# The first attention loads and row-maximum pieces placed inside the projections of a hybrid encoder layer

## The chip, the cores and the metric

The kernel runs on one NeuronCore of one Trainium2 chip. The metric is the device time of one execution in microseconds (us); less is better. TensorE (PE) multiplies, VectorE (DVE), ScalarE (ACT) and GpSimd (POOL) do the elementwise work, and SyncE (SP) issues nearly all DMA transfers from one in-order queue.

## The reference

One encoder layer runs on a prompt (1024 tokens) and on a sample (2048 tokens), each of width 1024, with 256 memory tokens each. Cut to what matters:

```python
h = rms_norm(x, norm_pre);  z = h @ w_in          # 1024 -> 2304 columns
u_pool, g_pool, q, k, v, g_attn, q_x, g_x = split(z)
pool_out = multiscale_pool(u_pool, pool_w, pool_scale) * silu(g_pool)      # windows 2, 4, 8, 16
q = apply_rope(rms_norm(q, q_norm));  k = apply_rope(rms_norm(k, k_norm))  # 8 query, 2 key heads of 64
attn_out = softmax(q @ k.T / 8) @ v * silu(g_attn)
k_m, v_m = split(rms_norm(mem, mem_norm) @ w_mem_kv)
x_out = softmax(q_x @ k_m.T / 8) @ v_m * silu(g_x)                         # 4 heads
y = concat(pool_out, attn_out, x_out) @ w_out
return x + rms_norm(y, norm_post)
```

All arithmetic is float32. The kernel reaches that on TensorE by splitting an operand into a high and a low part and adding three products (high by high, high by low, low by high).

## The kernel before, in words

**Phase 1, the projections (L72 to L427).** The tokens go through in super blocks `SB`: the memory tokens, the prompt (two blocks of 512 tokens), and two super blocks of two blocks each for the sample. For a super block the columns of `w_in` come in six groups of up to 384 columns, in the order of the list `tok_groups` (L377): `group_n0` (query heads), `ct[2]` (two gate chunks and the first memory-query chunk), `group_n1` (two query heads, keys, values), `ct[0]` (two pooling chunks and a gate chunk), `ct[1]` (gates), `ct[3]` (second memory-query chunk, two gate chunks). A `transposed` chunk makes 128 columns for 512 tokens by 24 matmuls into a PSUM tile `pz`; `natural` makes tokens by columns. Query and key heads are normalised, rotated on VectorE and POOL (`norm_rope`) and transposed on TensorE (`ptq`). Every result is stored to scratch in DRAM: queries (`dq`, `dqx`), keys (`dk`, `dkm`), values (`dv`, `dvm`), gates (`dg`, from tiles `gst`), pooled values (`dp`).

**Phase 2, attention and output (L430 to L878).** It opens pools of its own when the pools of phase 1 close. A *pair* is 256 queries (two tiles of 128); eight pairs of the sample are followed by four of the prompt. Each pair has three *groups*, of kind 0 and 1 (self attention, one key head each) and kind 2 (memory attention). A *slot* handles one chunk of 128 keys of one group. In a slot `weights` makes S by matmuls with the high part (`qa`, `KA`) and the low part (`qb`, `KB`), and ScalarE takes the exponential into a tile `P`; `sums` adds `P` to `z` (the sum over key chunks, so far 128 x 1024), columns up to `CUT` = 512 on POOL and the rest on VectorE (L613); `values` multiplies `P` by `V` into `acc`. At a group's end `totals` (L631) adds `z` over partitions by matmuls with `ones` into a PSUM tile `N`, `take` multiplies `acc` by the gate, `inverse` takes 1/z and sends it through DRAM (`rows`) to a broadcast tile `gz`, and `store_mix` (L657) multiplies on POOL (`o`, or `pu` for the pooled part), casts the high part of `mix` on ScalarE and subtracts the low part on POOL (L784).

The exponential needs a bound for each row beforehand. `largest` (L553) makes it in pieces, called *looks* here: the high-part product of 128 queries with 1024 keys into a PSUM tile `N`, reduced by VectorE (L570). When a group's pieces are through, `shift` (L574) transposes the negated maxima into a row of `qb`, so that S comes out shifted. A look stands some slots ahead of the slot that needs it; those that fall before slot 0, 20 pieces, are executed before it (L836 to L841).

The output projection of a finished pair is cut into pieces of three matmuls (L726 to L728), spread over the following slots (`HOLD` says when they may start). `Output` loads the rows of x (`xr`, L711), normalises, adds, and stores. For the last pair everything runs at the end. The table of what is due in which slot is written by hand; each engine's instructions stay in the order in which phase 2 writes them (`manual_schedule`). Phase 1's order is the scheduler's, and a tile in a reused place waits for the readers of what was there.

Of the kernel before, what the change touches and what calls it, by code (L numbers as in the profile page):

```python
# [23 lines left out]
def encoder(ctx, tc, I, O):  # L24
# [46 lines left out]

    with ExitStack() as p1:  # L72
# [3 lines left out]
        pst = p1.enter_context(tc.tile_pool(name="pst", bufs=2, space=PSUM))  # L76
# [15 lines left out]
        def hT_block(sb, blk):  # L92
# [4 lines left out]
            for i in range(4):  # L97
                x = two.tile([128, D], F32, name="x", tag="x", bufs=4)
                nc.sync.dma_start(out=x, in_=rows(sb, blk, i))
                if kind not in gains:  # L100
                    gains[kind] = one.tile([128, D], F32, name="gain", tag="gain")
                    src = I["mem_norm" if kind == "mem" else "norm_pre"]
                    nc.sync.dma_start(out=gains[kind], in_=src.broadcast_to([128, D]))
                junk = one.tile([128, D], mybir.dt.bfloat16, name="junk", tag="junk")
                ss = two.tile([128, 1], F32, name="ss", tag="ss")
                nc.scalar.activation(out=junk, in_=x, func=AF.Square, accum_out=ss)
                r = rsqrt(two, ss, 1, D, "rsx")
# [27 lines left out]
        def product(ps, terms):  # L135

            n = len(terms)
            for c, (sh, sl, mh, ml) in enumerate(terms):
                nc.tensor.matmul(ps, lhsT=sh, rhs=mh, start=c == 0, stop=False)  # L139
                nc.tensor.matmul(ps, lhsT=sh, rhs=ml, start=False, stop=False)  # L140
                nc.tensor.matmul(ps, lhsT=sl, rhs=mh, start=False, stop=c == n - 1)  # L141

# [9 lines left out]
        def transposed(hT, w, col):  # L152
# [3 lines left out]
            product(ps, [(w[0][:, c, f], w[1][:, c, f], hT[0][:, c], hT[1][:, c]) for c in range(NC)])  # L156
# [5 lines left out]
        def rope_tables():  # L162
            out = []
            raw = [two.tile([128, NTT, 64], F32, name="ropec", tag="ropec", bufs=1),
                   two.tile([128, NTT, 64], F32, name="ropes", tag="ropes", bufs=1)]
            for r, key in zip(raw, ("rope_c", "rope_s")):
                nc.sync.dma_start(out=r, in_=I[key])
            for key in ("k_norm", "q_norm"):
                g = one.tile([128, 2, 64], F32, name="hg", tag="hg" + key)
# [9 lines left out]
                for j in range(2):  # L179
                    if key == "q_norm":  # L180
                        t = raw[j]
                    else:
                        t = one.tile([128, NTT, 64], F32, name="ropek", tag=f"ropek{j}")
# [7 lines left out]
        def norm_rope(ps, parts, tt):  # L191
# [3 lines left out]
            z = two.tile([128, 384], F32, name="z", tag="z")  # L195
            sq = two.tile([128, 384], F32, name="sq", tag="sq")
            t1 = two.tile([128, 384], F32, name="t1", tag="t1")
            nc.scalar.copy(out=z[:, 0:w], in_=ps[:, 0:w])
            nc.scalar.activation(out=sq[:, 0:w], in_=ps[:, 0:w], func=AF.Square)
            ss = two.tile([128, 6], F32, name="ssh", tag="ssh")  # L200
# [3 lines left out]
            r = rsqrt(two, ss[:, 0:n], n, 64, f"rsh{n}")  # L204
# [22 lines left out]
        def heads_transposed(src, npair):  # L227
# [4 lines left out]
            o = two.tile([128, 2, 3, 128], F32R, name="qst", tag="qst")  # L232
# [7 lines left out]
        def group_n0(s, b, hT, w):  # L240
            if not rope:
                rope.update(zip("qk", rope_tables()))
# [10 lines left out]
        def group_n1(s, b, hT, w):  # L253
            for i in range(4):
                tt = 4 * b + i
                ps = natural(hT, w, i, 0, 384)
                vst = two.tile([128, 2, 64], F32, name="vst", tag="vst")
# [104 lines left out]
        def chunks_group(chunks):  # L362
            def run(s, b, hT, w):
                for k, (_, f, args) in enumerate(chunks):
                    f(s, b, *args, transposed(hT, w, 128 * k))
# [11 lines left out]
        tok_groups = [(w_in, [(512, 384)], group_n0), ct[2], (w_in, [(896, 384)], group_n1),  # L377
                      ct[0], ct[1], ct[3]]
# [12 lines left out]
        def mem_v(s, b, hT, w):  # L391
            for i in range(4):
                ps = natural(hT, w, i, 0, 256).rearrange("p (h d) -> p h d", d=64)
                vst = two.tile([128, 4, 64], F32, name="vmst", tag="vmst", bufs=1)
# [15 lines left out]

        for sb, (kind, s, nb, b0) in enumerate(SB):
            groups = groups_of(sb)
            nxt = []
            for gi, (src, pieces, run) in enumerate(groups):
# [15 lines left out]
    with ExitStack() as p2:  # L430
        def pool(name, bufs, space=bass.MemoryType.SB):
            return p2.enter_context(tc.tile_pool(name=name, bufs=bufs, space=space, reuse_waits="tile"))

        one = pool("p2one", 1)
        two = pool("p2two", 2)
        pss = pool("pss", 2, PSUM)
        psn = pool("psn", 2, PSUM)
        psa = pool("psa", 1, PSUM)
        pso = pool("pso", 1, PSUM)

        ones = one.tile([128, 32], F32, name="ones")
        nc.vector.memset(ones, 1.0)

        KA = [one.tile([128, 2048], F32R, name=f"KA{kind}") for kind in range(2)]
        KB = [one.tile([128, 2048], F32R, name=f"KB{kind}") for kind in range(2)]
        KA.append(one.tile([128, 2, 2, NMEM], F32R, name="KA2"))
        KB.append(one.tile([128, 2, 2, NMEM], F32R, name="KB2"))
        for t in KB:  # L450
            nc.vector.memset(t[64:65].bitcast(F32), 1.0)
        V = [one.tile([128, 16, 64], F32, name=f"V{kind}") for kind in range(2)]
        V.append(one.tile([128, 2, 4, 64], F32, name="V2"))
        has_K, has_V = set(), set()

        def load_K(s, kind):
            has_K.add((s, kind))
            for hl in range(2):
                for t, h in ((KA, 64 * hl), (KB, 0))[:2 - hl]:
                    if kind == 2:  # L460
                        src = DKM[hl, :, :, s].rearrange("d (c j) m -> d c j m", j=2)
                        nc.sync.dma_start(out=t[2][h:h + 64].bitcast(F32), in_=src)
                        continue
# [457 lines left out]
```

## Time and profile before

| | us |
|---|---|
| three runs | 1940.56, 1941.95, 1943.42 |
| median | 1941.95 |
| profiled execution, its own time | 1940.45 |
| span of the profiled execution | 1938.6 |
| TensorE busy | 1830.0 |
| VectorE busy | 1126.4 |
| ScalarE busy | 699.3 |
| POOL busy | 914.3 |

The span is what the profile covers, from the first to the last instruction; the execution's own time is 1.85 us longer. The page divides the span into 40 slices of 48.5 us and gives the busy tenths of each engine and the clock that TensorE was granted. A bracket behind an instruction of the timeline gives the idle time of its engine before it and what ended that time. Engines that are not the bound may be idle at no cost.

### The profile page before, as it was taken

Reading aid. Unit: us, or ns where it says so; the run is one execution under the profiler, and the core shown is the slowest. Engines: PE = TensorE matmul, PEld = TensorE weight load, DVE = VectorE, ACT = ScalarE, POOL = GpSimd, SP = SyncE. Lnnn points to the kernel's source line nnn. Section 1 sums busy time; section 2 is a strip of 40 time slices with the busy share of each in tenths; the row PEclk is TensorE's granted clock in tenths of the full one; section 3 lists DMA queues with packets and bytes.
Section 4 is the critical chain, followed back from the end, with each engine's and each line's share of the span. In section 5 each row is a group of like instructions: output and inputs, shape, how many; then the busy total and the mean of one; then the engine's idle time right before and its main releaser. Section 6 shows DMA issues by size and latency. Waiting matters only on the chain.

```text
span 1938.6 us, 23683 instructions
## 1 busy us (share of the span) xinstructions
PE 1830.0 (94%) x8520; PEld 1289.7 (67%) x8520; DVE 1126.4 (58%) x1304; ACT 699.3 (36%) x1266; POOL 914.3 (47%) x816
## 2 busy tenths in 40 slices
PE   7999999999999938999999999999999999999995
PEld 6998898978998824456565655656565655565564
DVE  6833254422623018876767677676767666756742
ACT  5522242313422102543434444443434443333331
POOL 3735033620634003863746456373746454635644
PEclk9999999999999967899999999999999999999998
DMA  6653355434443273212112021222212143323211
GB/s 235 200 147 89 110 161 138 116 100 123 118 123 86 66 176 118 82 39 77 60 47 80 26 79 44 77 60 77 61 48 78 49 125 83 93 77 104 82 39 60
DMA packets 148486, 181.84 MB, mean 94 GB/s; under 512 B 21504, under 2 KB 118416, under 8 KB 148368
## 3 DMA queue, kind: packets, MB, share of 16 engines
q1 hardware_dynamic: 148368, 180.33, 32.6%
q8 instruction: 67, 1.10, 0.2%
q14 instruction: 51, 0.42, 0.1%
HBM read 126.50 MB, written 53.62 MB: 93 GB/s over the span
## 4 chain that ended last, share of the span: by engine, by line
PE 70%; issue 10%; DVE 8%; POOL 6%; DMA 4%; ACT 2%; SPq 1%; POOLq 0%; ACTq 0%; DVEq 0%
PE acc L625 13%; PE S L595 11%; PE pz L141 9%; PE pz L139 9%; PE pz L140 9%; PE N L567 6%; PE py L726 3%; PE py L727 3%; PE py L728 3%; DVE nb L570 2%; POOL z L613 2%; DVE z L613 2%; PE S L599 1%; POOL rs L63 1%; PE N L633 1%
## 5 line engine op out<-in xcount | busy, mean ns | idle before, releaser
L602 ACT ACTIVATE P<-S 128x512 f32<-128x512 f32 x688 | 401.3, 599 | 612.8 <-PE S L595 435.4
L613 POOL TENSOR_TENSOR z<-z,P 128x512 f32<-128x512 f32 x272 | 389.2, 1431 | 260.3 <-ACT P L602 253.9
L570 DVE TENSOR_REDUCE nb<-N 128x1 f32<-128x1024 f32 x256 | 311.0, 1218 | 229.0 <-PE N L567 228.2
L625 PE MATMUL acc<-P,V 128*64 128x512 f32 (+1 forms) x1472 | 318.2, 574 | 0.5
L595 PE MATMUL S<-qa,KA 128*128 128x512 f32 x640 | 277.3, 433 | 11.6 <-ACT P L602 11.5
L613 DVE TENSOR_TENSOR z<-z,P 128x512 f32<-128x512 f32 x272 | 262.2, 964 | 15.9 <-ACT P L602 15.4
L567 PE MATMUL N<-KA,qa 128*128 128x512 f32 x640 | 217.0, 423 | 46.1 <-DMA qa<-dq 29.5
L595 PE MATMUL S<-qb,KB 65*128 65x512 f32 x640 | 255.2, 399 | 0.0
L139 PE MATMUL pz<-hT_hi,w_hi 128*128 128x512 f32 x592 | 233.2, 394 | 2.6 <-ACT w_hi L68 1.8
L140 PE MATMUL pz<-hT_lo,w_hi 128*128 128x512 f32 x592 | 233.9, 395 | 0.0
L141 PE MATMUL pz<-hT_hi,w_lo 128*128 128x512 f32 x592 | 232.3, 392 | 0.0
L595 PEld LDWEIGHTS S<-qa,KA 128*128 128x128 f32 x640 | 121.7, 190 | 146.4 <-issue 71.9
L625 PEld LDWEIGHTS acc<-P,V 128*64 128x64 f32 x1472 | 98.1, 137 | 177.6 <-issue 168.5
L567 PEld LDWEIGHTS N<-KA,qa 128*128 128x128 f32 x640 | 119.3, 198 | 97.5 <-DVE nb L570 35.1
L63 POOL TENSOR_TENSOR rs<-rs,mhalf 128x1 f32<-128x1 f32 (+2 forms) x100 | 92.9, 932 | 175.7 <-DVE rs L61 175.5
L570 DVE TENSOR_REDUCE top<-N 128x1 f32<-128x1024 f32 (+1 forms) x88 | 107.1, 1218 | 109.5 <-PE N L567 79.6
L613 POOL TENSOR_TENSOR z<-P 128x512 f32<-128x512 f32 x36 | 46.6, 1294 | 215.4 <-ACT P L602 154.3
L140 PE MATMUL pz<-w_lo,hT_hi 128*128 128x384 f32 (+1 forms) x416 | 140.5, 338 | 0.9 <-DVE w_lo L69 0.8
L141 PE MATMUL pz<-w_hi,hT_lo 128*128 128x384 f32 (+1 forms) x416 | 140.2, 338 | 0.0
L139 PE MATMUL pz<-w_hi,hT_hi 128*128 128x384 f32 (+1 forms) x416 | 139.4, 336 | 0.0
L726 PE MATMUL py<-wo_hi,mix 128*128 128x512 f32 x352 | 138.0, 392 | 0.0
L727 PE MATMUL py<-wo_lo,mix 128*128 128x512 f32 x352 | 137.2, 390 | 0.0
(115 smaller groups left out, 2587.5 us busy)
## 6 DMA issues: line engine op xcount, KB each, us to landing
wraw<-w_in SPq DMA_DIRECT2D x15, 1536.0 KB
dg<-gst SPq DMA_DIRECT2D x48, 256.0 KB
qa<-dq SPq DMA_DIRECT2D x48, 256.0 KB
gz<-rows SPq DMA_DIRECT2D x72, 128.0 KB
x<-x_sample SPq DMA_DIRECT2D x16, 512.0 KB
xr<-x_sample SPq DMA_DIRECT2D x16, 512.0 KB
y_sample<-xr SPq DMA_DIRECT2D x16, 512.0 KB
dq<-qst SPq DMA_DIRECT2D x48, 128.0 KB
```

The source lines that it names most:

```text
L63: nc.gpsimd.tensor_tensor(out=r, in0=r, in1=mhalf[:, 0:n], op=ALU.pow)
L139: nc.tensor.matmul(ps, lhsT=sh, rhs=mh, start=c == 0, stop=False)
L140: nc.tensor.matmul(ps, lhsT=sh, rhs=ml, start=False, stop=False)
L141: nc.tensor.matmul(ps, lhsT=sl, rhs=mh, start=False, stop=c == n - 1)
L567: nc.tensor.matmul(S[:, 512 * b:512 * b + 512], lhsT=q, rhs=KA[self.kind][:, k:k + 512], start=True, stop=True)
L570: nc.vector.tensor_reduce(out=out, in_=S, axis=AX.X, op=ALU.max, negate=True)
L595: nc.tensor.matmul(S, lhsT=K[self.kind][rows_, keys], rhs=q, start=n == 0, stop=n == 1)
L602: nc.scalar.activation(out=self.P[k][:, j], in_=S, func=AF.Exp)
L613: e.tensor_tensor(out=z[:, x], in0=a[:, x], in1=P[:, x], op=ALU.add)
L625: nc.tensor.matmul(self.acc[64 * j:64 * j + 64, x], lhsT=v, rhs=P[:, j, x], start=(k, i) == (0, 0), stop=k == self.chunks - 1, skip_group_ ...
L726: nc.tensor.matmul(ps, lhsT=mh, rhs=wo_hi[:, c, cols], start=first, stop=False)
L727: nc.tensor.matmul(ps, lhsT=mh, rhs=wo_lo[:, c, cols], start=False, stop=False)
```

## The change

The diff moves the classes `Group`, `Pair` and `Output`, the tables of slots and the first-load functions ahead of phase 1, and changes this:

- The six column groups come in the order keys and values, pooling, queries, gates: `group_n1`, `ct[0]`, `group_n0`, `ct[2]`, `ct[1]`, `ct[3]`.
- In the last super block, when the fourth group begins, the pools of x rows, heads and their PSUM tiles close, and two new ones open in their place: `early` (KA, KB0, KB2, qa, qb, the maxima) and `psn` (two PSUM tiles `N`). The loads of KA and qa of the first three groups are issued there.
- The 20 looks stand in the last group: `product` calls `look_ahead` after every second of its eight steps (six matmuls).
- KB is loaded by `shift`, no more by `load`. KB1, V, the output weights, `ones` and `npost` get their place behind the end of the projections.
- The cut of the z additions is indexed by the sequence: 0 for the prompt, which leaves all 1024 columns to VectorE and no instruction to POOL, and 512 for the sample as before.
- The first pair's products for `mix` may come from slot 12 on instead of slot 0.
- The last pair's two `Output` tiles take `xr` and `y` from the places of `P`, and `start`, which loads `xr`, is called at the tile's first output matmul.

```diff
-        tok_groups = [(w_in, [(512, 384)], group_n0), ct[2], (w_in, [(896, 384)], group_n1),
-                      ct[0], ct[1], ct[3]]
+        tok_groups = [(w_in, [(896, 384)], group_n1), ct[0], (w_in, [(512, 384)], group_n0),
+                      ct[2], ct[1], ct[3]]
...
+                last = sb + 1 == len(SB)
+                if last and gi == 3:
+                    front.close()
+                    early = ctx.enter_context(tc.tile_pool(name="early", bufs=1, side="right", reuse_waits="tile"))
+                    open_early()
+                    for g in loads.pop(-1):
+                        g.load()
+                if last and gi == 3:
+                    heads.close()
+                    psn = ctx.enter_context(tc.tile_pool(name="psn", bufs=2, space=PSUM, side="right", reuse_waits="tile"))
...
-                    run(s, b0 + blk, cur[blk], w)
+                    if last and final:
+                        with tc.manual_schedule(engines={mybir.EngineType.PE}):
+                            run(s, b0 + blk, cur[blk], w, look_ahead)
+                    else:
+                        run(s, b0 + blk, cur[blk], w)
...
+    def look_ahead():
+        if ahead:
+            g, n = ahead.pop(0)
+            g.largest(n)
...
+        def product(ps, terms, beside=lambda: None):
+                if c % 2:
+                    beside()
...
         def shift(self):
+            load_K(self.s, self.kind, KB, 0, 0)
...
-    CUT = 512
+    CUT = (0, 512)
...
+            cut = CUT[self.s]
+            if cut:
+                nc.gpsimd.tensor_tensor(out=z[:, :cut], in0=a[:, :cut], in1=P[:, :cut], op=ALU.add)
+            nc.vector.tensor_tensor(out=z[:, cut:], in0=a[:, cut:], in1=P[:, cut:], op=ALU.add)
...
+        free = 12 if pair is pairs[0] else first[pair.groups[0]] + HOLD[pair.s]
...
         def start(self):
+            tag = dict(tag="P", bufs=6) if self.last else dict(tag="xr", bufs=1)
+            self.xr = dbl.tile([128, D], F32, name="xr", **tag)
             nc.sync.dma_start(out=self.xr, in_=I[("x_prompt", "x_sample")[s]][0, 128 * t:128 * t + 128])
...
         def piece(self, h, c, first, final):
             if self.last:
                 if self.both is None:
+                    self.start()
```

In the order of TensorE's instructions, before, the end of the projections (`pz`) is followed by all looks ahead (`N`, 44 matmuls) and then the first S:

```order
L140 MATMUL pz<-hT_lo,w_hi 128x512
L141 MATMUL pz<-hT_hi,w_lo 128x512
L567 MATMUL N<-KA_5966,qa 128x512 x28
L559 MATMUL N<-KA_5970,qa 128x256 x8
L567 MATMUL N<-KA_5966,qa 128x512 x4
L567 MATMUL N<-KA_5967,qa 128x512 x4
L599 MATMUL S<-qa,KA_5970 128x256 x2
```

After the change the looks stand between projection matmuls of the last group; this is one of them (the line numbers are those of the changed file):

```order
L549 MATMUL pz<-hT_lo,w_hi 128x512
L550 MATMUL pz<-hT_hi,w_lo 128x512
L191 MATMUL N<-KA_5428,qa 128x512 x2
L548 MATMUL pz<-hT_hi,w_hi 128x512
L549 MATMUL pz<-hT_lo,w_hi 128x512
```

And behind the last `pz` matmul the first S follows directly:

```order
L550 MATMUL pz<-hT_hi,w_lo 128x512
L224 MATMUL S<-qa,KA_5429 128x256 x2
L224 MATMUL S<-qb,KB_5430 128x256 x2
L191 MATMUL N<-KA_5428,qa 128x512 x2
L224 MATMUL S<-qa,KA_5429 128x256 x2
```

The 20 looks have left the place between the projections and the first S. In SP's queue, before, the first loads stand behind the last stores of gates (`dg`), with the V, gate and pool loads right behind them:

```order
L465 DMA KA_5966<-dk_114 64x1024 x2
L465 DMA KB_5968<-dk_114 64x1024 x2
L465 DMA KA_5966<-dk_114 64x1024 x2
L537 DMA qa<-dq_0_0_75 64x1024 x2
L537 DMA qb<-dqx_0_79 64x1024
L537 DMA qb<-dq_0_0_75 64x1024
L471 DMA V_5977<-dvm_119 128x512
L549 DMA gate<-dg_0_3_83 128x2x128 x2
L678 DMA pg<-dg_0_0_80 128x2x128 x2
```

After, the KA and qa loads stand between the gate stores of the fourth group of the last super block:

```order
L754 DMA dg_3_2_109<-gst 512x1x128
L99 DMA KA_5428<-dk_114 64x1024 x4
L161 DMA qa<-dq_0_1_76 64x1024 x2
L96 DMA KA_5429<-dkm 64x4x256 x2
L161 DMA qa<-dqx_0_79 64x1024 x2
L99 DMA KA_5426<-dk_114 64x1024 x4
L161 DMA qa<-dq_0_0_75 64x1024 x2
L754 DMA dg_3_2_109<-gst 512x1x128
```

and behind the last gate stores of the projections only this is left of them:

```order
L754 DMA dg_3_3_110<-gst 512x1x128 x2
L104 DMA V_6123<-dvm_119 128x512
L173 DMA gate<-dg_0_3_83 128x2x128 x2
L305 DMA pg<-dg_0_0_80 128x2x128 x2
L306 DMA pu<-dp_112 128x2x256
L107 DMA V_6121<-dv_116 128x512 x2
```

KA and qa have moved ahead by more than two column groups; V, the gate and the pooled rows have stayed behind the projections. On POOL, the last pair's instructions before:

```order
L661 TENSOR_TENSOR o<-o,gz 128x512
L613 TENSOR_TENSOR z<-z,P 128x512
L755 TENSOR_TENSOR xr<-xr,y 128x1024
L613 TENSOR_TENSOR z<-z,P 128x512
L784 TENSOR_TENSOR mix<-pu,mix 128x512
L784 TENSOR_TENSOR mix<-o,mix 128x512 x2
```

and after:

```order
L288 TENSOR_TENSOR o<-o,gz 128x512
L386 TENSOR_TENSOR xr<-xr,y 128x1024
L416 TENSOR_TENSOR mix<-pu,mix 128x512
L416 TENSOR_TENSOR mix<-o,mix 128x512 x2
L288 TENSOR_TENSOR o<-o,gz 128x2x2x128
```

The z additions have left POOL; on VectorE the same places now read `z<-z,P 128x1024` instead of `128x512`.

More of the change, by code (lines that the diff above doesn't have):

```diff
@@ new lines, in encoder, with at @@
+    CUT = (0, 512)
+    HOLD = (16, 26)
+    LEAD, RUN = 4, 4
+    pairs = [Pair(s, p) for s in (1, 0) for p in range(SEQS[s][1] // 256)]
+    groups = []
+    for pair in pairs:
+        kinds = (2, 0, 1) if pair is pairs[0] else (0, 2, 1)
+        pair.groups = [Group(len(groups) + n, pair.s, pair.p, kind) for n, kind in enumerate(kinds)]
+        groups += pair.groups
+    slots = [(g, k) for g in groups for k in range(g.chunks)]
+    later = {}
+    END = 0.5
+    def at(slot, f, *args):
+        later.setdefault(slot, []).append((f, args))
@@ new lines, in due, with open_fill @@
+    def due(slot):
+        for f, args in later.pop(slot, ()):
+            f(*args)
+    first = {}
+    for n, (g, k) in enumerate(slots):
+        first.setdefault(g, n)
+    fill, until = [], [0]
+    def open_fill(pair, slot):
+        fill.extend(pair.todo())
+        n = pairs.index(pair) + 1
+        until[0] = first[pairs[n].groups[0]] + HOLD[pairs[n].s] if n < len(pairs) else slot
+    for pair in pairs:
+        ends = [first[g] + g.chunks - 1 for g in pair.groups]
+        at(min(ends), pair.load_pool)
+        free = 12 if pair is pairs[0] else first[pair.groups[0]] + HOLD[pair.s]
+        at(max(min(ends) + 4, free), pair.pool, max(min(ends) + 4, free))
+        for g in pair.groups:
+            wait = max(first[g] + g.chunks + 5, free)
+            at(wait + END, g.mix_out, wait + END, pair)
+        at(max(ends) + 9, open_fill, pair, max(ends) + 9)
@@ new lines, in encoder @@
+    for g in groups:
+        n, c = first[g], g.chunks
+        at(n + END, g.load_late)
+        for k in range(0, c, RUN):
+            ks = list(range(k, min(k + RUN, c)))
+            at(n + ks[-1] + 1 + END, g.values, ks)
+        at(n + c + 1 + END, g.totals)
+        at(n + c + 2, g.take)
+        at(n + c + 2 + END, g.inverse)
+    for c in range(NC):
+        at(4 + 3 * c, load_w_out, c)
+        at(7 + 3 * c, split_w_out, c)
+    at(7 + 3 * NC, load_npost)
+    looks, n = {}, len(slots)
@@ new lines, in encoder @@
+    left = {g: list(range(len(g.pieces))) for g in groups}
+    while any(left.values()):
+        n -= 1
+        able = [g for g in groups if left[g] and first[g] - LEAD > n]
+        if able:
+            looks[n] = (able[0], left[able[0]].pop())
+    ahead = [looks[n] for n in sorted(looks) if n < 0]
+    loads = {}
+    for n, (g, k) in looks.items():
+        if k == 0:
+            loads.setdefault(max(n - 3, -1), []).append(g)
+    order = {mybir.EngineType.PE, mybir.EngineType.Activation, mybir.EngineType.DVE,
+             mybir.EngineType.Pool}
@@ L409, in encoder @@
         rope = {}
+        early = psn = None
         for sb, (kind, s, nb, b0) in enumerate(SB):
@@ new lines, in pool @@
+    def pool(name, bufs, space=bass.MemoryType.SB):
+        return ctx.enter_context(tc.tile_pool(name=name, bufs=bufs, space=space, reuse_waits="tile"))
+    own = pool("p2one", 1)
+    dbl = pool("p2two", 2)
+    pss = pool("pss", 2, PSUM)
+    psa = pool("psa", 1, PSUM)
+    pso = pool("pso", 1, PSUM)
+    ones = own.tile([128, 32], F32, name="ones")
+    nc.vector.memset(ones, 1.0)
+    KB[1] = own.tile([128, 2048], F32R, name="KB1")
+    nc.vector.memset(KB[1][64:65].bitcast(F32), 1.0)
+    V += [own.tile([128, 16, 64], F32, name=f"V{kind}") for kind in range(2)]
```

720 lines of the change are left out of this document (323 added, 397 removed).

## The prediction

> **What bounds the kernel now.** I read the page's first two parts, then the clock and work by stretch, then TensorE's instructions around the one stretch in which it stands still, then its waits in the prompt pairs, and the last 50 us.
>
> ```profile
> span 1938.6 us, 23683 instructions
> PE 1830.0 (94%) x8520; PEld 1289.7 (67%) x8520; DVE 1126.4 (58%) x1304; ACT 699.3 (36%) x1266; POOL 914.3 (47%) x816
> ...
> PE   7999999999999938999999999999999999999995
> ...
> PEclk9999999999999967899999999999999999999998
> ```
>
> TensorE is the bound: 1830.0 of 1938.6 us busy. The tenths show three weak places: the first slice, slices 15 and 16 (about 680 to 780 us, where the clock drops too), and the last. The change touches the middle one and the last; the prompt pairs before the end lose a little in pieces too short for a tenth.
>
> The stretches around slice 15 (busy us and count for each engine, then granted clock, DMA share, GB/s):
>
> ```profile
> 659.00:692.00 33.00, 32.77 (x145) 26.82 (x143) 5.99 (x8) 3.72 (x7) 0.00 (x0) 1.00 0.24 64
> 692.00:721.00 29.00, 0.00 (x0) 0.00 (x0) 0.00 (x0) 1.74 (x2) 0.00 (x0) 0.54 0.99 209
> 721.00:746.00 25.00, 22.83 (x44) 11.23 (x45) 22.14 (x22) 0.00 (x0) 0.00 (x0) 0.50 0.69 199
> ...
> 1737.00:1812.00 75.00, 70.42 (x327) 44.87 (x328) 46.51 (x48) 28.12 (x53) 39.65 (x27) 0.98 0.31 89
> ```
>
> From 692 to 721 us nothing computes and the DMA engines are full. From 721 to 746 the 20 first looks run at half clock. The last row is one whole prompt pair, used below. TensorE at both ends of the hole:
>
> ```profile
> 691.38 0.39 PE L141 MATMUL pz<-hT_hi,w_lo 128*128 128x512 f32 x1
> 721.23 0.80 PE L567 MATMUL N<-KA,qa 128*128 128x512 f32 x1 [29.46 <-DMA qa<-dq]
> ...
> 746.24 0.63 PE L599 MATMUL S<-qa,KA 128*128 128x256 f32 x2
> ...
> 749.15 0.41 PE L599 MATMUL S<-qa,KA 128*128 128x256 f32 x2
> ...
> 752.09 1.08 PE L625 MATMUL acc<-P,V 128*64 128x256 f32 x8
> ```
>
> The last projection matmul ends at 691.77; the first look waits 29.46 us for its queries; the first S of slot 0 starts at 746.24. So 54.5 us lie between the last projection and the first slot, and only the 20 looks happen in them. The matmuls of the projection follow each other every 33.00 / 145 = 0.227 us at full clock (first row of the stretches).
>
> **Term 1: loads and looks inside the projections.** The loads of KA and qa now stand in SP's queue three groups (about 100 us) before the end of the projections, and the 20 looks stand between projection matmuls in the last group. Each look is two 512-column matmuls (or four of 256), 0.45 us at full clock, so 9.1 us for 20. The last projection then ends at 691.77 + 9.1 = 700.9, with S directly behind. Against 746.24 that is 45.3 us; the third S block, which waits for the first exponential, confirms it. On ScalarE there stand:
>
> ```profile
> 691.86 0.60 ACT L342 ACTIVATE gst<-pz 128x512 f32<-128x512 f32 x1 [4.84 <-PE pz L141]
> 692.47 1.28 ACT L602 ACT_TABLE_LOAD   x1
> ```
>
> After the last projection come the last gate (to 0.7 us behind its end) and the table load (to 1.98): the exponentials start near 702.9, and the third S block, which takes the buffer of the first, some 0.6 us later, at 703.5 instead of 749.15, 45.7 earlier. I take 45.7.
>
> VectorE has room for the looks: it is busy 5.99 of 33 us in the last group, and the looks' reductions, 22.14 us in the third row, are spread over it, one every six projection matmuls, 6 x 0.227 + 0.45 = 1.8 us. The loads have 66 us after their issue until the last group, and DMA is at 0.24 there. What the cover hides is thus the full 29 us of DMA time; if the loads were late, the looks would stall the projection (third rival).
>
> What is late next: the loads that stay behind the last projection matmul (their pool opens there), and the ones row of KB1 on VectorE.
>
> ```profile
> 715.21 0.32 SPq L471 DMA_DIRECT2D V<-dvm  x1
> 716.50 1.51 SPq L549 DMA_DIRECT2D gate<-dg  x2
> 718.92 1.51 SPq L678 DMA_DIRECT2D pg<-dg  x2
> ...
> 682.75 1.76 DVE L451 MEMSET KB<- 1x2048 f32 x1 [0.46 <-issue]
> ```
>
> V2 stands on SP behind the store of the last gate (which ends at 702.0), so it issues near 702.6 and lands near 705 to 706 (an estimate: the x row of 512 KB in term 5 is issued at 1930.38 and ends the wait at 1933.70, 3.3 us); the first acc comes 752.09 - 746.24 = 5.9 us after the first S, 706.8. It fits by 1 to 2 us. V2's own issue, the gate's and the pool gate's take 0.32 + 1.51 + 1.51 = 3.3 us of SP, and pu a little, so V0 issues near 706.5 and lands by 710; the first acc on V0 stands four chunks behind the one on V2, near 712 (an estimate at the same distance of 5.9 us). The KB1 memset, 1.76 us, lies between two reductions of the running looks. I charge 2 us for the memset and these near misses; bounds 0 (all hidden) and 6 (V2 late by 3 and V0 by 3). Term 1: -43.7, from -46 to -39.
>
> **Term 2: the first pair's mix from slot 12.** Before, at slot 0's end:
>
> ```profile
> 773.89 0.62 ACT L784 CAST mix<-o 128x512 fp32r<-128x512 f32 x1 [3.43 <-POOL o L661]
> ...
> 775.06 0.50 PE L595 MATMUL S<-qa,KA 128*128 128x512 f32 x1 [2.14 <-ACT P L602]
> ```
>
> ScalarE's cast waits 3.43 us for POOL's product; the exponentials queue behind it, and TensorE loses 2.14. With the product placed later it should be done before the cast's turn. I take -1.5, bounds -2.1 and +1 (the wait meets another slot).
>
> **Term 3: z of the prompt on VectorE alone.** The diff also makes the cut 0 for the prompt: all 1024 columns of each add go to VectorE, none to POOL. In a prompt pair now:
>
> ```profile
> 1752.00 0.39 PE L595 MATMUL S<-qb,KB 65*128 65x512 f32 x1
> 1755.62 0.76 PE L633 MATMUL N<-z,ones 128*32 128x256 f32 x8 [3.23 <-POOL z L613]
> 1756.31 0.80 PE L595 MATMUL S<-qa,KA 128*128 128x512 f32 x1
> ...
> 1751.55 2.35 POOL L755 TENSOR_TENSOR xr<-xr,y 128x1024 f32<-128x1024 f32 x1
> 1753.86 1.71 POOL L613 TENSOR_TENSOR z<-z,P 128x512 f32<-128x512 f32 x1
> ...
> 1748.69 1.75 DVE L613 TENSOR_TENSOR z<-z,P 128x512 f32<-128x512 f32 x1
> ...
> 1766.55 0.68 DVE L613 TENSOR_TENSOR z<-z,P 128x512 f32<-128x512 f32 x1
> ...
> 1870.12 1.29 DVE L752 SCALAR_TENSOR_TENSOR y<-y,rs,npost 128x1024 f32<-128x1024 f32 x1 [0.66 <-POOL rs L63]
> ...
> PE N L633 <- POOL z L613: 16.9, 5, 6.6
> ```
>
> VectorE finishes its half of the last add at 1750.44; POOL, behind the residual add of 2.35 us, finishes its half at 1755.57. The total waits for POOL alone. In this answer the columns are start, us, engine, line; the last row is of the waits from 1600 us on (us in total, times, longest). On VectorE the wide add costs about 1.29 us with nothing beside it (the row of width 1024) and up to 2 x 1.75 = 3.5 by the contended row; I take 1.29 to 1.8, nearest to the 1.29 row, since POOL has fewer instructions left to meet. The last add then ends at 1750.5 to 1752.2, and the total starts right behind the S matmuls, 1752.23. That is 3.2 us per pair, in the three pairs with this wait (16.9 less the 6.6 of the last pair and 0.7 of the first leaves 9.6): -9.6. VectorE does 15 adds per pair; by the two rows of halves and the row of 1.29 each costs 0.6 us more (alone) to 1.75 more (always contended), 9 to 26 us beside 46.51 of 75: off the bound, at the worst end only just. Bounds: 0, if VectorE's reductions come late by what the totals gain, and -14, as below.
>
> After the wait of 3.23 us the matmuls of 1756.31 run for 0.80 us each against 0.39 ahead of it, so the clock has halved for some microseconds, which would give 1.5 us more per pair. "TensorE: Matmul & The Clock Gate" of the Trainium skill, Part 1, says that the clock is cut after an idle window of about 3.4 us and comes back after as long a busy one. By it, a wait of 3.23 us would often cost nothing more and the sum stays -9.6; by the row the wait costs 4.7 and the sum would be -14. The measured 25 us at 0.50 from 721 to 746, with TensorE busy 22.83 of them, also don't agree with a return after one busy window. I keep -9.6, because the next S is held by ScalarE and VectorE soon after.
>
> **Term 4: last pair's total.** The end before:
>
> ```profile
> 1899.65 0.65 PE L633 MATMUL N<-z,ones 128*32 128x256 f32 x4 [6.58 <-POOL z L613]
> ...
> 1890.94 3.47 POOL L661 TENSOR_TENSOR o<-o,gz 128x512 f32<-128x512 f32 x2
> ...
> 1896.04 2.33 POOL L755 TENSOR_TENSOR xr<-xr,y 128x1024 f32<-128x1024 f32 x1
> 1898.34 1.26 POOL L613 TENSOR_TENSOR z<-z,P 128x512 f32<-128x512 f32 x1
> 1899.56 1.26 POOL L784 TENSOR_TENSOR mix<-pu,mix 128x512 fp32r<-128x512 f32 x1
> ```
>
> Without POOL's two adds the product, the residual and the low part of the first mix follow at once: 1890.94 + 3.47 + 2.33 + 1.26 = 1898.0 instead of 1900.8. The total itself could run at 1893.1 (6.58 earlier), but the third matmul of the output projection, 2.0 us behind the total, needs that low part: it starts at 1898.0 instead of 1901.7. So the gain is not 6.6 but about 4: -4.0, bounds -2.5 and -6.6.
>
> **Term 5: the last tile's x row.** At the very end:
>
> ```profile
> 1928.24 1.41 DVE L752 SCALAR_TENSOR_TENSOR y<-N,rs,npost 128x512 f32<-128x512 f32 x2
> ...
> 1930.38 0.34 SPq L711 DMA_DIRECT2D xr<-x_prompt  x1
> ...
> 1933.70 1.77 POOL L755 TENSOR_TENSOR xr<-xr,y 128x512 f32<-128x512 f32 x1 [6.12 <-DMA xr<-x_prompt]
> ```
>
> The load now stands ahead of the stores and lands early. The adds then start when y is made (1928.9 and 1929.65) and end at 1930.4 to 1930.9 instead of 1935.47: -4.6, bounds -3.5 and -5.
>
> **Term 6: the new column order.** The same matmuls run; what changes is the neighbours. The queries' group now comes behind the pooling chunks, whose POOL chain has waits of its own:
>
> ```profile
> 608.74 1.06 POOL L304 TENSOR_TENSOR s<-s 128x525 f32<-128x525 f32 x1 [6.48 <-DMA dp<-s]
> ...
> PE ptq L231 <- DVE t L221: 2.8, 5, 1.5
> ```
>
> The queries' rotation on POOL stands in order behind these, and the transposes on TensorE behind the rotation. Four projection buffers and the group's other matmuls cover most of it. I take +1; bounds -3 (the present transposes of the queries wait 2.8 us in all, second row, of the waits up to 692 us, and may no more) and +13, two thirds of the 6.48 in each of three super blocks.
>
> **Sum.** -43.7 - 1.5 - 9.6 - 4.0 - 4.6 + 1 = -62.4 against the profiled execution's own 1940.45: 1878.0. The median of the runs stands 1.5 above that execution, so 1879.
>
> **Rivals.**
> - *The wide add gives nothing* (0.10). What VectorE's contended row shows, 1.75 against 0.68, would hold for every wide add, 3.5 us: the last add of a pair ends at 1752.2 plus the delay of those before it, and the reductions of the looks come late. Terms 3 and 4 go: 1879 + 13.6 = 1893. "SBUF — State Buffer" of the Trainium skill, "Who interferes with whom", says that a VectorE instruction with two SBUF inputs and a POOL instruction that reads SBUF exclude each other for the whole instruction, the first one holding it; this speaks against wider adds while POOL still multiplies and adds, and the trace's two rows agree. For it: POOL's o and xr work remains. Against: POOL loses half its 39.65 us per pair, so an add meets it less often.
> - *The pooling chain stalls the queries* (0.10). Term 6 at its upper bound, +13: 1891.
> - *The early loads don't come early* (0.03). If KA or qa are held by the stores queued ahead, the looks stall the projections by what is now 29.46 us, and of term 1 remain 54.5 - 29.46 - 9.1 = 16 us, less 2: 1879 + 43.7 - 14 = 1909. Against it: issue 66 us ahead, DMA share 0.24.
> - *Slower than before* (0.02): VectorE becomes the bound of the prompt pairs. It has 75 - 46.51 = 28.5 us free per pair. To undo the 48.8 us of the other terms over four pairs and pass 0.2% it must add 28.5 + 13 = 42 us a pair, 2.8 us for each of 15 adds; the contended rows give 1.75 at most. It decides only above 2.8, so it hardly can.
>
> **How the numbers follow.** The forecast that all six terms come about as sized has 0.75, 1871 to 1887 by itself: about half of the terms' bounds on either side. The range must take in one of the rivals of 0.10, with both at 1891 to 1893: 1866 to 1895. Low end: all terms at their better bounds but term 6, 1879 - 13. A change of less than 0.2%, 4 us, is about what a measurement of this kernel can't tell from none; only a case far from all of these would land there, 0.01; slower 0.02, faster 0.97.
>
> **What would show it.** In the changed profile: no wait of over 2 us for queries ahead of a look, clock 1.0 through the last group and the first slots, S of slot 0 near 701. No wait of TensorE for POOL's z from 1590 on; wide adds at 1.3 to 1.8 us. The last total 6 us nearer to its acc, with a wait for the low mix right behind. No x row behind a y store. The prediction is wrong if TensorE waits for V, if the projections take over 8 us more, or if the looks wait for VectorE inside the last group.

## The result, and the profile after

The changed kernel takes 1885.3 us (median of four runs, 1880.81 to 1887.28) against 1941.49 before: a ratio of 0.9706, 95% interval 0.9687 to 0.9725. Its profiled execution took 1885.09, 55.4 us less than that of before; 62.4 were forecast. The page after (span, busy time, busy tenths and clock):

```profile
span 1883.0 us, 23531 instructions
...
PE 1816.8 (96%) x8520; PEld 1282.0 (68%) x8520; DVE 1131.4 (60%) x1304; ACT 697.3 (37%) x1266; POOL 856.7 (45%) x756
...
PE   7999999999999998999999999999999999999996
...
PEclk9999999999999999999999999999999999999998
```

The hole in slices 15 and 16 is gone, with its clock. TensorE at the place where it was, after:

```profile
698.26 0.40 PE L550 MATMUL pz<-hT_hi,w_lo 128*128 128x512 f32 x1
698.49 0.40 PE L224 MATMUL S<-qa,KA 128*128 128x256 f32 x2
...
701.30 0.51 PE L224 MATMUL S<-qa,KA 128*128 128x256 f32 x2 [1.17 <-ACT P L227]
...
704.34 1.95 PE L252 MATMUL acc<-P,V 128*64 128x256 f32 x16
...
714.31 3.65 PE L252 MATMUL acc<-P,V 128*64 128x512 f32 x16
```

S follows the last projection matmul without a gap; the only wait is 1.17 us for the first exponential, and no acc waits for V. Through the last group with its looks (659 to 699 us) TensorE was busy 40.00 of 40.00 us, at a granted clock of 1.00. All matmul groups `totals` (36 of them) can be set side by side in the two traces by their start. That gives where the 55.6 us of span came from (the starts before and after in brackets):

| stretch | forecast | measured |
|---|---|---|
| start to the first total (755.57, 707.82) | terms 1 and 6: -42.7 | -47.75 |
| to the third total (848.39, 796.97) | term 2: -1.5 | -3.7 |
| to the last total of the sample (1607.87, 1557.10) | 0 | +0.65 |
| to the last total but one (1866.34, 1817.06) | term 3: -9.6 | +1.5 |
| to the last output matmul (1923.31, 1872.18) | term 4: -4.0 | -1.85 |
| to the end of the span (1938.6, 1883.0) | term 5: -4.6 | -4.5 |

The sum came within 7 us, from terms that missed in both directions: the early start is worth more than forecast, the wide addition in the three prompt pairs nothing. The same prompt pair as in the prediction, after. TensorE:

```profile
1701.37 0.64 PE L260 MATMUL N<-z,ones 128*32 128x256 f32 x8 [0.33 <-DVE top L194]
...
1704.77 0.74 PE L183 MATMUL N<-KA,qa 128*128 128x256 f32 x4 [0.58 <-DVE top L194]
...
1708.40 1.22 PE L191 MATMUL N<-KA,qa 128*128 128x512 f32 x2 [1.96 <-DVE rz L272]
```

VectorE:

```profile
1697.90 2.29 DVE L240 TENSOR_TENSOR z<-z,P 128x1024 f32<-128x1024 f32 x1
1700.11 2.34 DVE L194 TENSOR_REDUCE top<-N 128x1 f32<-128x1024 f32 x2
1702.37 1.21 DVE L240 TENSOR_TENSOR z<-P 128x1024 f32<-128x1024 f32 x1
...
1705.99 0.69 DVE L266 TENSOR_TENSOR o<-acc,gate 128x512 f32<-128x512 f32 x1 [1.28 <-POOL mix L416]
1706.60 1.75 DVE L272 RECIPROCAL rz<-N 128x256 f32<-128x256 f32 x1
```

POOL:

```profile
1699.06 3.35 POOL L386 TENSOR_TENSOR xr<-xr,y 128x1024 f32<-128x1024 f32 x1
1702.37 2.34 POOL L416 TENSOR_TENSOR mix<-pu,mix 128x512 fp32r<-128x512 f32 x1
1704.67 2.52 POOL L416 TENSOR_TENSOR mix<-o,mix 128x512 fp32r<-128x512 f32 x2
```

The total's wait has fallen from 3.23 to 0.33 us as forecast. Seven us later the look waits 1.96 for the reciprocal, which frees its PSUM tile. The reciprocal stands behind the gating (`o<-acc,gate`), which waits 1.28 us for POOL's low part to be through with an older `o`. POOL is late there because its residual add takes 3.35 us beside VectorE's wide add (2.35 before) and its first low part 2.34 beside the next one (1.27 before). The clock then halves: two 512-column matmuls take 1.22 us, and the next acc takes 5.55 in the following pair against 3.65 above:

```profile
1785.21 5.55 PE L252 MATMUL acc<-P,V 128*64 128x512 f32 x16
```

From total to total the three pairs lose 1.9, 3.3 and 4.2 us behind the 2.5 that each total gained. At the end, TensorE and POOL:

```profile
1844.94 0.64 PE L260 MATMUL N<-z,ones 128*32 128x256 f32 x8 [1.39 <-DVE z L240]
1848.38 0.79 PE L359 MATMUL N<-wo_hi,mix 128*128 128x512 f32 x1 [2.14 <-POOL mix L416]
...
1843.77 3.34 POOL L386 TENSOR_TENSOR xr<-xr,y 128x1024 f32<-128x1024 f32 x1
1847.07 1.26 POOL L416 TENSOR_TENSOR mix<-pu,mix 128x512 fp32r<-128x512 f32 x1
```

The wait for the low part is the one that the prediction named. The same matmul, the third of the output projection, stood here before:

```profile
1901.68 0.63 PE L728 MATMUL N<-wo_hi,mix 128*128 128x512 f32 x1
```

### The profile page after: what moved, and what is told of

The parts are those of the page before. It is cut to its first block, busy times and chain, and to the rows that moved or that the text cites. A ratio compares the mean times of both kernels' runs of the same rounds, so it can differ in the third digit from the quotient of the medians.

```text
span 1883.0 us, 23531 instructions
## 1 busy us (share of the span) xinstructions
PE 1816.8 (96%) x8520; PEld 1282.0 (68%) x8520; DVE 1131.4 (60%) x1304; ACT 697.3 (37%) x1266; POOL 856.7 (45%) x756
## 5 line engine op out<-in xcount | busy, mean ns | idle before, releaser
L239 POOL TENSOR_TENSOR z<-z,P 128x512 f32<-128x512 f32 x224 | 316.9, 1415 | 223.7 <-ACT P L227 218.8
L240 DVE TENSOR_TENSOR z<-z,P 128x512 f32<-128x512 f32 (+1 forms) x272 | 273.6, 1006 | 12.7 <-ACT P L227 12.3
L63 POOL TENSOR_TENSOR rs<-rs,mhalf 128x1 f32<-128x1 f32 (+2 forms) x100 | 100.4, 1007 | 386.2 <-DVE rs L61 386.1
L191 PE MATMUL N<-KA,qa 128*128 128x512 f32 x640 | 208.1, 406 | 18.4 <-DVE rz L272 11.7
L357 PE MATMUL py<-wo_hi,mix 128*128 128x512 f32 x352 | 137.7, 391 | 0.0
L359 PE MATMUL py<-wo_hi,mix 128*128 128x512 f32 x352 | 137.4, 390 | 0.0
```

Source lines behind the costliest of these rows:

```text
L191: nc.tensor.matmul(S[:, 512 * b:512 * b + 512], lhsT=q, rhs=KA[self.kind][:, k:k + 512], start=True, stop=True)
L239: nc.gpsimd.tensor_tensor(out=z[:, :cut], in0=a[:, :cut], in1=P[:, :cut], op=ALU.add)
L240: nc.vector.tensor_tensor(out=z[:, cut:], in0=a[:, cut:], in1=P[:, cut:], op=ALU.add)
L357: nc.tensor.matmul(ps, lhsT=mh, rhs=wo_hi[:, c, cols], start=first, stop=False)
```

## The experiments

Times are medians of their runs; ratios are to the kernel before. In the order in which they ran.

**cut512.** The change with the z additions of the prompt shared again.

```diff
-    CUT = (0, 512)
+    CUT = (512, 512)
```

> The changed kernel with z of the prompt again half on POOL, half on VectorE. Theory A (the wait moved): each prompt pair is held by VectorE and POOL together, and the 2.5 us that the total gained in the changed kernel were given back 10 us later in a wait for the reciprocal plus a slow clock in the next acc; undoing the cut then brings the wait of 3.2 us for POOL's z back and takes the 2.0 us wait for the reciprocal away, and the three pairs together move by -2 to +1 us. The last pair loses about 2, the whole run stays at 1885 +- 3. Theory B (the prediction's third and fourth terms): the three pairs lose 9.6 and the last one 2 to 4, so 1897 to 1899.

Measured: 1887.04, ratio 0.9716 (0.9703 to 0.973), 1.7 above the change. The waits of TensorE in the whole span (us in all, times, longest):

```profile
PE N L260 <- POOL z L239: 20.3, 6, 6.6
...
PE N L191 <- DVE rz L272: 6.0, 10, 0.6
```

The totals wait 3.2 us for POOL again and the longest wait for the reciprocal is 0.6. Between the third total and the last but one this kernel is 1.6 us faster than the change; the last total then comes 5.4 us later. Theory A: in the three pairs the wide add had only moved the wait.

**mix_slot0.** The change with the first pair's products from slot 0.

```diff
-        free = 12 if pair is pairs[0] else first[pair.groups[0]] + HOLD[pair.s]
+        free = 0 if pair is pairs[0] else first[pair.groups[0]] + HOLD[pair.s]
```

> The changed kernel with the first pair's products allowed from slot 0 again. From the distance between the totals of the first three groups, the later products are worth 3.7 us net in the changed kernel. Theory A (POOL is short in the first 36 slots, and what moves later leaves it free for z): 3 to 4 us slower than the changed kernel, about 1889, with ScalarE's wait for POOL's product back. Theory B (the gain there came from V and weights landing at another time): same as the changed kernel within 1 us up to the third total.

Measured: 1897.06, ratio 0.9768 (0.9754 to 0.9781); 11.8 above the change and more than either theory had. In the traces the second and the third total each come 4.0 us later than in the change, 8.0 in all; of the rest 1.7 lie in the prompt pairs, which the edit doesn't touch. SP, POOL, ScalarE and TensorE at the place:

```profile
719.36 0.55 SPq L274 DMA_DIRECT2D rows<-rz  x1
725.09 1.10 SPq L278 DMA_DIRECT2D gz<-rows  x2
...
728.94 1.26 POOL L288 TENSOR_TENSOR o<-o,gz 128x512 f32<-128x512 f32 x1 [3.52 <-DMA gz<-rows]
...
730.24 0.62 ACT L416 CAST mix<-o 128x512 fp32r<-128x512 f32 x1 [6.49 <-POOL o L288]
...
731.40 0.79 PE L220 MATMUL S<-qa,KA 128*128 128x512 f32 x1 [5.19 <-ACT P L227]
```

The broadcast of the reciprocals is issued 5.7 us behind its rows (1.75 before, 761.20 to 762.95), POOL waits for it, ScalarE's cast waits 6.49 for POOL, and the exponentials stand behind the cast: TensorE loses 5.19 instead of the 2.14 of before. With the early start this wait is longer, and slot 12 takes it away.

**looks_behind.** The change with the 20 looks behind the projections instead of between their matmuls.

```diff
-                            run(s, b0 + blk, cur[blk], w, look_ahead)
+                            run(s, b0 + blk, cur[blk], w)
...
     with tc.manual_schedule(engines=order):
+        while ahead:
+            look_ahead()
         slot = 0
```

> The changed kernel with the 20 looks behind the last projection matmul instead of between them; loads stay early. Theory A (first term in two parts, load time 29.5 and the looks' own 25 us, which VectorE's reductions of 1.22 us set): the last projection ends near 689.4, the looks take 20 reductions, about 24 us, S of slot 0 at 713 to 715, 15 us later than in the changed kernel; about 1900. Theory B (the looks were slow before because TensorE's clock was halved after the 29 us of nothing): at full clock behind the projections they need 10 to 12 us, S at 700 to 702, 1887.

Measured: 1906.45, ratio 0.9809 (0.9793 to 0.9825). The stretch of the looks (busy and count by engine, clock, DMA), and its end:

```profile
689.00:716.00 27.00, 21.27 (x48) 10.62 (x47) 24.07 (x24) 1.88 (x2) 0.00 (x0) 0.62 0.62 175
...
716.10 0.63 PE L224 MATMUL S<-qa,KA 128*128 128x256 f32 x2
```

S comes at 716.10, 17.6 us later than in the change: VectorE is busy 24.07 of the 27 us with the reductions and a memset of 1.76, so it sets the pace, as theory A has it; the clock is halved here too, but VectorE waits only 0.18 us for each two looks. The profiled execution took 1900.53, as forecast by theory A, and so did one other of the five runs (1900.92); the other three took 1906.5 to 1907.1, and what they spent 6 us more on isn't known. So the first term is two things: the early loads take away the wait of 29.5 us (the first look runs at 689.57, right behind the last projection), and standing between projection matmuls hides another 17.6 us.

**o_in_gate.** The change with the gating written over the gate's tile, so that the next gating doesn't wait for POOL to be through with the old one.

```diff
-            self.gate = dbl.tile([128, 2, 2, 128], F32, name="gate", tag="gate")
+            self.gate = dbl.tile([128, 2, 2, 128], F32, name="gate", tag="gate", bufs=4)
...
-            self.o = dbl.tile([128, 512], F32, name="o", tag="o")
-            nc.vector.tensor_tensor(out=self.o, in0=self.acc,
-                                    in1=self.gate.rearrange("p i t q -> p (i t q)"), op=ALU.mult)
+            self.o = self.gate.rearrange("p i t q -> p (i t q)")
+            nc.vector.tensor_tensor(out=self.o, in0=self.acc, in1=self.o, op=ALU.mult)
```

> The changed kernel with the gated result written over the gate's own tile, four buffers of it instead of two of gate and two of o, so that the gating on VectorE no more waits for POOL's low part of the mix of two groups before. Theory A (in a prompt pair VectorE waits 1.3 us for POOL's mix, the reciprocal comes late by that, the look waits 2.0 us for the reciprocal, and the clock halves): the wait of 2.0 falls to under 0.8, the slow acc behind it (5.3 us against 3.6) goes, and the three pairs gain 2 to 3 us each, 6 to 9 in all: 1876 to 1879. Theory B (the wide add itself makes VectorE late): the gating starts earlier but the reciprocal is late nonetheless, and the pairs gain under 1 us each: 1882 to 1885.

Measured: 1880.88 (1880.62 to 1881.38), ratio 0.9683 (0.967 to 0.9697). VectorE and TensorE in the pair shown above:

```profile
1703.36 0.68 DVE L266 TENSOR_TENSOR gate<-acc,gate 128x512 f32<-128x512 f32 x1
1703.95 1.74 DVE L271 RECIPROCAL rz<-N 128x256 f32<-128x256 f32 x1
...
1705.75 1.09 PE L191 MATMUL N<-KA,qa 128*128 128x512 f32 x2 [0.59 <-DVE rz L271]
```

The gating waits for nothing and the look 0.59 instead of 1.96. The three pairs gain 2.3, 1.85 and 0.4 us, 4.5 in all, between the two forecasts: the chain of theory A is there, its price is smaller. In the pair shown the clock still halves (1.09 for two matmuls) after short waits. In the third pair the look waits 0.59 too and the clock stays full; but 10 us later S waits for the row of maxima in `qb`, whose transfers SP issues behind the broadcast of the reciprocals, then 1.41 us for an exponential, and the clock halves there:

```profile
1789.02 0.48 PE L224 MATMUL S<-qb,KB 65*128 65x256 f32 x2 [0.76 <-DMA qb<-rows]
```

**order_alone.** The kernel before with the new column order only.

```diff
-        tok_groups = [(w_in, [(512, 384)], group_n0), ct[2], (w_in, [(896, 384)], group_n1),
-                      ct[0], ct[1], ct[3]]
+        tok_groups = [(w_in, [(896, 384)], group_n1), ct[0], (w_in, [(512, 384)], group_n0),
+                      ct[2], ct[1], ct[3]]
```

> The kernel before with the new column order alone (the rotation tables made in the keys' group, since that comes first). Theory A (the queries' transposes behind the pooling chunks wait less, 0.8 instead of 2.8 us): the last projection matmul ends at 689.4 +- 0.5 instead of 691.77, and everything behind it keeps its distance; 1939 to 1940. Theory B (the prediction's sixth term): +1 us. Theory C (part of the 2.4 us came from the looks being cheaper than 9.1 us): the projections end at 691 to 692.

Measured: 1942.28, ratio 1.0004 (0.9995 to 1.0013): no difference. (The edit also makes the rotation tables in the keys' group, which now comes first.) Its last projection ends at 690.29, 1.5 earlier, but the kernel before_mix12 below, with the old order, ends its own at 688.81. What the order does to the projections is inside what one trace differs from another.

**o_in_gate_cut512.** Both edits, o_in_gate and cut512.

> The kernel o_in_gate with z of the prompt half on POOL again. Theory A (two waits in series: the total's for POOL's z, then the gating's for POOL's mix; the cut takes away the first, the gate buffers the second): with the cut undone the totals wait 3.2 us for POOL's z again and the gate buffers bring nothing, since the gating is never late behind that wait; the three pairs and the last one are as in cut512, so 1886 to 1888. Theory B (the buffers were the whole gain and the cut is worth nothing): 1880 to 1882, as o_in_gate.

Measured: 1886.08, ratio 0.9717 (0.9704 to 0.9731), 5.2 above o_in_gate and 1.0 below cut512. So the wide add is worth 5.2 us once the gating doesn't wait, in the three pairs and the last one together (in the two traces 3.2 and 3.4 us, of which 1.1 went on a later start). The gate buffers are worth 1.0 at most without it: two waits in series, theory A.

**gate_lastwide.** o_in_gate with only a group's last add wide.

```diff
-            cut = CUT[self.s]
+            cut = CUT[self.s] if self.s or k < self.chunks - 1 else 0
...
-    CUT = (0, 512)
+    CUT = (512, 512)
```

> The kernel o_in_gate with only the last add of each prompt group 1024 wide on VectorE, the others half and half. Theory A (what still holds a prompt pair in o_in_gate is VectorE, 22 of 28 us busy behind the total, waits of 0.6 us for reductions and reciprocals, and the clock drops after them): with less on VectorE the three pairs come 1 to 2 us each earlier; 1876 to 1879. Theory B (POOL, busy again, is late with the add before the last one, and VectorE waits for it): the totals wait 1 to 2 us and the run is at 1881 to 1885.

Measured: 1887.18, ratio 0.972 (0.9707 to 0.9733). The waits of TensorE in the prompt:

```profile
PE N L260 <- DVE top L194: 10.2, 3, 3.4
```

VectorE's wide add now needs POOL's half of the add before it: in one pair it waits 2.40 us for it, then takes 3.38 beside POOL's residual add, and the reductions queue behind that. TensorE waits 3.4 us at each total. Theory B, with a worse price.

**gate_mix20.** o_in_gate with the first pair's products from slot 20 (`free = 20`).

> The kernel o_in_gate with the first pair's products from slot 20 instead of 12. Theory A (the 3.3 us wait of the second group's total for POOL's z is made by the products and low parts that POOL does in that group): the wait goes and the third total comes 3 us earlier; 1877 to 1879. Theory B (the splits of the output weights on POOL make it): the wait stays within 1 us, 1880 to 1882.

Measured: 1877.57 (1876.7 to 1878.31), ratio 0.9671 (0.9658 to 0.9684). The 3.3 us wait of the second total is gone, but the third total comes 0.7 later than in o_in_gate, net of that: a wait of 2.2 for a reduction and a slow clock give it back. The gain stands in the second and third of the three prompt pairs (1.5 and 2.95 us), which the edit doesn't touch. In the second, after the same waits as in o_in_gate, the clock stayed full:

```profile
1707.38 0.73 PE L191 MATMUL N<-KA,qa 128*128 128x512 f32 x2 [0.59 <-DVE rz L271]
```

In the third, S waits at most 0.2 us for the row of maxima and 0.77 for the exponential behind it, where o_in_gate waits 0.76 and 1.41, and the clock stays full there too. The time is as forecast by theory A, its reason isn't.

**x_late.** The change with the last pair's x rows and y in their single place again, loaded when the output pieces are through.

> The changed kernel with the last pair's x rows and y back in their single place, loaded only when the output pieces are through. Theory A (fifth term): the second tile's x row is again issued behind the stores of the first, its adds wait about 4 us, and the span from the last output matmul to the end grows from 10.4 to 14.9 us: 4.5 us slower than the changed kernel, 1888 to 1890. Theory B (the stores of the first tile, not the x row, set the end): 1 us or less, 1885 to 1886.

Measured: 1889.95, ratio 0.9737 (0.9724 to 0.9749), 4.6 above the change. SP and POOL:

```profile
1880.07 0.34 SPq L340 DMA_DIRECT2D xr<-x_prompt  x1
...
1883.50 1.77 POOL L385 TENSOR_TENSOR xr<-xr,y 128x512 f32<-128x512 f32 x1 [6.21 <-DMA xr<-x_prompt]
```

Theory A.

**before_mix12.** The kernel before with the first pair's products from slot 12.

> The kernel before with the first pair's products from slot 12 instead of slot 0, nothing else. Theory A (the products wait for transfers: in the changed kernel slot 0 starts while the first loads still run, and there the late products are worth 8 us; before, the loads had landed in the hole of 29 us): about 2 us faster than before, 1939 to 1940, a 2.1 us wait less. Theory B (the price is POOL's order, whenever the loads land): 7 to 9 us faster, 1932 to 1934.

Measured: 1936.65, ratio 0.9979 (0.9969 to 0.9988). From the first to the third total it gains 2.9 us; another 2.15 lie ahead of the first total, where nothing was changed. Nearer to theory A: the late products are worth 3 us before and 8 in the change, where the early slots meet the loads.

**gate_mix20_xdve.** gate_mix20 with one residual add, that of the last but one pair's second tile, on VectorE behind a gating instead of on POOL ahead of the last pair's low parts.

```diff
+                if self.pair is pairs[-2] and self.x:
+                    held.append((add, nc.vector, c))
+                else:
+                    add(nc.vector if h else nc.gpsimd, c)
...
+            while held:
+                f, *args = held.pop()
+                f(*args)
```

> The kernel gate_mix20 with the residual add of the last but one pair's second tile put on VectorE behind the last gating but one, instead of on POOL ahead of the last pair's low parts. Theory A (fourth term: the total comes 6 us earlier, but the third output matmul waits 2.1 us for the pooled low part, which stands behind that add of 3.3 us on POOL): the wait goes, and the clock is back earlier; 2 to 3 us faster than gate_mix20, 1874.5 to 1876. Theory B (the high part's cast on ScalarE is late too): the wait moves there and the run stays at 1877 to 1878.

Measured: 1874.53 (1871.98 to 1877.58), ratio 0.966 (0.9646 to 0.9675): the fastest of all, 10.8 below the change and 3.0 below gate_mix20, though the runs of the two overlap. In the traces the 3.0 lie behind the last total. The third output matmul of the last pair, then the ninth, the only one that still waits:

```profile
1838.80 0.49 PE L362 MATMUL N<-wo_hi,mix 128*128 128x512 f32 x1
...
1841.02 0.50 PE L362 MATMUL N<-wo_hi,mix 128*128 128x512 f32 x1 [0.57 <-POOL mix L424]
```

The third waited 2.13 us in gate_mix20 and waits for nothing now; the ninth waits 0.57 for the next low part. The clock stays full here, where in gate_mix20 it was halved for 3.4 us: theory A.

## Why the prediction was right, and where not

That the time came within 7 us is in part luck: the start gained 5 us and term 2 another 2 more than forecast, and terms 3 and 4 missed their sum by 13.

**Term 1** held, in both halves, by looks_behind: 30 us of loads and 17.6 us of looks. The loads were issued 25 to 38 us ahead of the first look (619.5 to 632.5, against 657.7) and not the 66 of the prediction, and that was enough. The 2 us charged for V and the memset weren't spent there: acc waited for nothing, and TensorE met no wait for VectorE in the first 10 us. Of the 5 us by which the start did better than terms 1 and 6, up to 3 may be the trace of before: the same projections ended at 691.77 in it and at 688.81 in before_mix12.

**Term 6** was forecast at +1, with -3 to +13 around it; order_alone shows no difference. The rival of a pooling chain that stalls the queries is out.

**Term 2** was sized from the wait as it stood before, -1.5. Alone it is worth 3, and inside the change 8 (mix_slot0), where the slots start 48 us earlier and the products meet the loads: that wait is 5.19 us instead of 2.14, which is 3 of the 5 us between the two; the other 2 were not traced. The step that failed was to price an edit by a row of the old surroundings while another term changed them. The table's -3.7 is the gain of 8.0 less 4.3 that the early start costs between the first and the third total (848.39 - 755.57 = 92.8 before, 97.1 in mix_slot0).

**Term 3** is the step that was wrong, and +1.5 lies outside its bounds of 0 and -14: "the next S is held by ScalarE and VectorE soon after" was given as a reason to leave the clock out, and not followed to the work that holds it. The totals did gain, 2.5 us each where the sum had 3.2. But POOL's low parts, VectorE's gating, the reciprocal and the look's PSUM tile were next in line, hidden until then by the 3.23 us for which all waited. The cut serves terms 3 and 4 together, forecast at -13.6: without the gate buffers it is worth 1.7 (cut512 against the change, in a spread of 6), with them 5.2. For these two terms that is the outcome of the first rival; its mechanism is half of it. The rows bear out "SBUF — State Buffer" of the Trainium skill, "Who interferes with whom": where VectorE's wide add came first it took 1.21 us and POOL's low part beside it 2.34 instead of 1.27, and where POOL's product came first it took 2.29, and POOL's residual add beside it 3.35 instead of 2.35. Most wide adds took 1.22, less than the 1.29 to 1.8 of the prediction, and VectorE itself had room, 49.6 of 74 us by the same pair's window.

**Term 4** had the right wait, and up to the third output matmul it came as sized: from the last total but one that matmul stands 35.3 us before (1866.34 to 1901.68) and 31.3 after (1817.06 to 1848.38), -4.0. This was luck in part: POOL's products and residual add took 4.09 and 3.34 where the sum had 3.47 and 2.33 from the rows of before, but POOL also began them 1.9 us earlier. The step that failed is again the clock. Behind the waits of 1.39 and 2.14 us the matmuls ran at half speed (0.63 us) until 1853.67, 5.3 us behind the third; before, until 1902.53, 0.9 behind it. These 4.4 us at half speed cost 2.2, and -1.85 is left. **Term 5** came as forecast.

In the prediction's range one sum is off: the better bounds of terms 1 to 5 add up to 10 us, not 13, so the low end should have been 1869.

**The clock after waits that are alike.** In o_in_gate and gate_mix20 the waits ahead of the same look are 0.33, 0.6 and 0.6 us in both, and it runs at 1.09 in one and 0.73 in the other. The granted clock in these traces changes only at points that lie whole multiples of 3.41 us apart, and the sum of TensorE's idle time between two such points goes with the change. Two of these stretches for each kernel, first o_in_gate, then gate_mix20 (TensorE's busy time is the first number behind the comma, the granted clock the one behind POOL's):

```profile
1702.51:1705.92 3.41, 2.23 (x11) 1.33 (x10) 3.41 (x4) 2.13 (x4) 3.40 (x3) 1.00 0.47 166
1705.92:1709.33 3.41, 3.41 (x8) 1.40 (x10) 3.38 (x4) 0.60 (x1) 0.00 (x0) 0.50 0.86 263
...
1703.07:1706.48 3.41, 2.80 (x16) 2.06 (x15) 3.41 (x4) 1.80 (x4) 3.41 (x3) 1.00 0.40 153
1706.48:1709.90 3.42, 2.83 (x14) 1.22 (x14) 3.38 (x4) 1.56 (x3) 1.06 (x1) 1.00 0.79 233
```

In o_in_gate both waits of 0.59 fall into one stretch, 1.18 us idle, and the next runs at half clock. In gate_mix20 a border falls between them, about 0.6 idle on each side, and the clock stays full. "TensorE: Matmul & The Clock Gate" of the Trainium skill, Part 1, has a free-running window, by which equal waits can end differently, and these rows agree; but it speaks of an idle window of about 3.4 us, and here 1.18 of 3.41 were enough. So the 1.5 us that gate_mix20 gained in the second pair hang on where the borders fell. **Open:** what sets the borders in an execution, and why the row of maxima came earlier in the third pair of gate_mix20, where it gained 2.95.

## What to carry to other kernels

Loads and reductions that only the next stage needs can stand between the matmuls of the last one, and gain twice: the transfer's time, and the time of the engine that reduces. Behind a wait that is removed, follow the chain of all that waited along with it, buffers included, up to the next instruction of the bound engine; only the difference is the gain. Price an edit in the surroundings that the other edits leave, not in the old ones. Add to a wait what the slow clock behind it costs, and add up short waits that stand close together.

## What the runs showed of the hardware that was not expected

TensorE's clock was halved behind waits much shorter than the 29 us hole: behind one of 1.96 us, and behind two of 0.59 within 3.41. In all 13 traces of this case the granted clock changes only at multiples of 3.41 us from its other changes. At full clock, a stretch between two such points in which the trace shows TensorE idle for 1.6 us or more was followed by half clock 78 times of 84 (the other six at 75 us or in the last 20); with less than 1.1 idle, never in 6844; between, 6 times of 34. The way back needed nearly gapless work: a half-clock stretch with less than 0.05 us idle was followed by full clock in all 61 cases, one with 0.4 or more once in 81, one between in 9 of 38. So in looks_behind the looks ran at 2.35 us for four matmuls, half speed, for 16 us, with waits of only 0.19 us between them:

```profile
699.84 2.35 PE L191 MATMUL N<-KA,qa 128*128 128x512 f32 x4 [0.19 <-DVE nb L194]
```
